# The last expert of each mixture layer is weighted in one operation and scattered by itself

## The chip, the cores and the metric

The kernel runs on one core of a Trainium2 chip. A core has a matrix engine (PE; its weight loads are listed apart as PEld), a vector engine (DVE), a scalar engine (ACT), a general engine (POOL), a queue engine (SP) and 16 DMA engines. Each engine works through its own list of instructions in order. The metric is the time of one execution on the device, in microseconds (us); the median of several executions counts.

## The reference, cut to what matters

Two transformer blocks are computed in float32 on 256 tokens of width 1024 (and 256 context tokens). The second block has two layers, l = 0 and l = 1, and each ends in a mixture of 16 experts. Every expert takes its 32 best tokens, runs them through its own three matrices, and adds the gated result back to those tokens:

```python
gate, idx = lax.top_k(jnp.swapaxes(aff, 1, 2), cap)      # cap = 32 of 256 tokens
xe = h[bidx, idx]
hid = jax.nn.silu(xe @ w1) * (xe @ w3)                    # per expert
ye = (hid @ w2) * gate[..., None]
return jnp.zeros_like(h).at[bidx, idx].add(ye)            # and x = x + g2 * this
...
x = x + g2 * expert_choice_ffn(h2, ...)
if need_ctx: xc = xc + g2c * expert_choice_ffn(hc2, ...)  # layer 0 only
return rms_norm(x, final_norm)
```

In layer 0 the experts run for two streams, x and the context xc (`ns == 2`). In layer 1 they run for x alone (`ns == 1`), and the block ends with the norm.

## The kernel before

The function `moe` builds a mixture layer and `run` executes it. A loop runs over the 16 experts. Each needs 12 MB of weights (w1, w3, w2, four transfers of 1 MB each, tile `wm`), loaded through a ring of buffers by SP. The products with them (`ps_a<-wm,xe`, `ps_a<-wm,xf`, `ps_a<-wm,hidT`) use groups of the array's columns: 64 columns per stream pair in layer 0 (two products side by side), 32 in layer 1 (four side by side). `hid` (L1325) is the gated hidden state, made when w1 and w3 of an expert are done; its transpose `hidT` feeds w2; the result of w2 stands in `py`, with 32 rows for each part of the width and each stream.

L1344 multiplies `py` by the layer's gate vector G2 into the tile `ye`, in four operations of 32 rows, because each expert has its own 32 rows of `ye` (four experts fill 128 rows). After every fourth expert `gates(qt)` builds the four experts' scatter matrix: a comparison on DVE (L1228, tile `Pg`), a product on POOL (L1230), transposes on PE, and a copy to `PgT`. The scatter then multiplies `PgT` and `ye` over all 128 rows, 512 columns at a time (`ps_b<-ye,PgT`): eight products in layer 0 and four in layer 1. L1360 adds them to the streams on DVE. In layer 0 each group of four is added to x and xc at once; in layer 1 the four groups gather in four banks `acc`, and the add comes behind the last group, at e == 15.

Behind layer 0 comes the odd layer's input: `normed` squares xc and x on ACT (L447), makes `rs` on POOL (L439) and `xn` on ACT and DVE (L170, L172); `mod_T` transposes `xn` on PE and splits the result into `oT` on ACT, DVE and POOL (L472 to L477). The first weights of that layer (`w<-in_odd_w_in`) are split on ACT and DVE or POOL (`wh`, L203, L205). Behind layer 1 comes the final norm (L1833 to L1840): squares on ACT, products with the norm's weights on POOL (first half of the tokens) and DVE (second half), `rs` on POOL, a scaling (L170, L172), and the stores.

The order of the instructions on each engine is set by a scheduler which simulates the program when it is built, not by the order of the code alone. Two helpers, `evac` and `scaled`, take ACT and DVE in turn, so one more call changes the engine of every later one.

Of the kernel before, what the change touches and what calls it, by code (L numbers as in the profile page):

```python
# [27 lines left out]
OP = mybir.AluOpType  # L28
# [85 lines left out]
def kernel(ctx, tc, A, out, dbg=None):  # L114
    nc = tc.nc
    dbg = dbg or {}
    V, S, G, PE = nc.vector, nc.scalar, nc.gpsimd, nc.tensor
# [19 lines left out]
    def ps_(tag):  # L137
        return PS["pool"].tile([128, 512], F32, name="ps_" + tag, tag=tag, bufs=PS["n"][tag])

    def psa():  # L140
        return ps_("a")

    def psb():
        return ps_("b")
# [3 lines left out]
    def mm(o, l, r, start=True, stop=True, **kw):  # L148
        PE.matmul(o, l, r, start=start, stop=stop, **kw)  # L149
# [3 lines left out]
    def evac(o, i):  # L153
        flip_eng[0] ^= 1
        if flip_eng[0]:
            S.activation(o, i, AF.Copy)
        else:
            V.tensor_copy(o, i)
# [19 lines left out]
    def bcast(ap, shape):  # L178
        return ap.to_broadcast(shape)
# [73 lines left out]
    def tr(o, i):  # L253
        n = i.shape[0]
        PE.transpose(o, i, ident[:n, :n])  # L255
# [120 lines left out]
    def in_pairs(j, n=128):  # L376

        c = 256 * (j // 2) + j % 2
        return slice(c, c + 2 * n - 1, 2)
# [790 lines left out]
    def moe(l, streams, stk):  # L1170

        ns = len(streams)
        nj = 4 // ns
        W = 32 * ns
        N = 1024 // nj
# [19 lines left out]
        G2 = SC.rearrange("p a b c -> p (a b c)")[:, 0:N]  # L1195
# [3 lines left out]
        def chosen(part, of=tuple(reversed(range(ns)))):  # L1199

            if part not in xe:
                inputs(part)
                P = mp.tile([128, ns, 2, 4, 32], F32, name="P", tag="P")
                for s in range(ns):
                    Ps[s, part] = P[:, s]
            for s in of:
                P = Ps[s, part]
                for t in range(2):
                    V.tensor_tensor(P[:, t], bcast(iota1[:, None, :], [128, 4, 32]),
                                    bcast(POS[s][:, t, 4 * part:4 * part + 4, None], [128, 4, 32]), op=OP.is_equal)  # L1210
                    V.tensor_scalar(P[:, t], P[:, t], QS[s][:, t:t + 1], None, op0=OP.mult)

        def gather(s, part, k, ps=None):

            ps = (ps_("g" if ns == 2 else "a")[:, 0:128] if ps is None else ps).rearrange("p (e w) -> p e w", w=32)
            for t in range(2):
                mm(ps, streams[s][:, t, in_pairs(k)], Ps[s, part][:, t], start=t == 0, stop=t == 1)
            affine(xe[part][:, k, :, 32 * s:32 * s + 32], ps, MS[:, i_sc, k, s:s + 1], shift[:, k, s:s + 1])

        def gates(qt):  # L1220

            p = psa() if ns == 1 else psb()
            for s in range(ns):
                Pg = rowp.tile([128, 512], F32, name="Pg", tag="r")
                for t in range(2):
                    g_ = Pg[:, 128 * t:128 * t + 128].rearrange("p (e w) -> p e w", w=32)
                    e4 = slice(4 * qt, 4 * qt + 4)
                    V.tensor_tensor(g_, bcast(iota1[:, None, :], [128, 4, 32]),  # L1228
                                    bcast(POS[s][:, t, e4, None], [128, 4, 32]), op=OP.is_equal)
                    G.tensor_tensor(g_, g_, bcast(AFF[s][:, t, e4, None], [128, 4, 32]), op=OP.mult)  # L1230
                    tr(p[:, 256 * s + 128 * t:256 * s + 128 * t + 128], Pg[:, 128 * t:128 * t + 128])
            PgT = rowp.tile([128, 512], F32, name="PgT", tag="r")
            evac(PgT[:, 0:256 * ns], p[:, 0:256 * ns])
            return PgT
# [29 lines left out]
        def ffn(lhs, src, before=None, last=False):  # L1264
            ps = psa()
            for kk in range(4):
                w = load_m(src, 2 * kk, last and kk == 3)
                for k in range(2):
                    if before and 2 * kk + k + 1 < 8:
                        before(2 * kk + k + 1)  # L1270
                    for j in range(nj):
                        mm(ps[W * j:W * j + W, :N], lhs(2 * kk + k), w[:, k, N * j:N * j + N],
                           start=kk == 0 and k == 0, stop=kk == 3 and k == 1)
            return ps
# [11 lines left out]
        def run():  # L1286
            yes = {}
            if ns == 1:
                acc = [psb() for j in range(4)]

            def work(name, n):
                return rowp.tile([128, 512], F32, name=name, tag="r")[:, :n]

            chosen(0, (0,))


            late = [(s, part, k) for part in ((1, 3, 2) if ns == 2 else (1, 2, 3)) for k in range(8) for s in range(ns)]
            turn = [0.0]

            def first(k):  # L1300
                if k < 7:
                    gather(0, 0, k + 1)

            def more(_):
                if late and e >= ((0, 1, 4, 3) if ns == 2 else (0, 1, 1, 1))[late[0][1]]:
                    turn[0] += 0.8
                    if turn[0] >= 1.0:
                        turn[0] -= 1.0
                        s, part, k = late.pop(0)
                        if part not in xe:  # L1310
                            chosen(part)
                        gather(s, part, k)

            gather(0, 0, 0)
            first(0)
            for e in range(16):
                def xk(k):
                    return xe[e // 4][:, k, e % 4]

                hook = more if e else first  # L1320
                p1 = ffn(xk, A["moe_w1_2"][l, e], hook)
                hid = work("hid", N)
                S.activation(hid, p1[:, :N], AF.Silu)  # L1323
                p3 = ffn(xk, A["moe_w3_2"][l, e])
                V.tensor_tensor(hid, hid, p3[:, :N], op=OP.mult)  # L1325
                nblk = N // 128
                pt = psa() if ns == 1 else ps_("t")
                for c in range(nblk):
                    tr(pt[:, 128 * c:128 * c + 128], hid[:, in_pairs(c)])
                hidT = work("hidT", N).rearrange("p (c w) -> p c w", c=nblk)  # L1330
                evac(hidT, pt[:, :N].rearrange("p (c w) -> p c w", c=nblk))

                py = ffn(lambda K: hidT[:, K % nblk, W * (K // nblk):W * (K // nblk) + W], A["moe_w2_2"][l, e],
                         more, last=e == 15)
                if e == 0:
                    gate2()
                if e == 0 or ns == 2 and e % 4 == 0:
                    xe["y"] = mp.tile([128, 2048], F32, name="ye", tag=("ye", "xf2")[e // 4 % 2])
                    ye = yes[e // 4] = xe["y"].rearrange("p (s n) -> p s n", s=2)
                o = 32 * (e % 4)  # L1340
                for j in range(nj):
                    for s in range(ns):
                        i = 32 * (ns * j + s)
                        V.tensor_tensor(ye[o:o + 32, s, N * j:N * j + N], py[i:i + 32, :N], G2[i:i + 32, :], op=OP.mult)  # L1344

                qt = (e + 1) // 4 - 1 if ns == 1 or e > 5 else 0
                if e % 4 < 3 and (ns == 1 or e != 5) or ns == 2 and e == 3:
                    continue
                assert ns == 1 or not late
                PgT = gates(qt)  # L1350
                for s in reversed(range(ns)):
                    for t in range(2):
                        for h in range(2):
                            ps = acc[2 * t + h] if ns == 1 else psb()
                            mm(ps, PgT[:, 256 * s + 128 * t:256 * s + 128 * t + 128],
                               yes[qt if ns == 2 else 0][:, s, 512 * h:512 * h + 512],
                               start=ns > 1 or e == 3, stop=ns > 1 or e == 15, skip_group_check=ns == 1)
                            if ns > 1 or e == 15:
                                d = streams[s][:, t, 512 * h:512 * h + 512]
                                V.tensor_tensor(d, d, ps, op=OP.add)  # L1360
            stk.close()

        return run, gts, apart_, slots, ahead


# [500 lines left out]
```

## Time and profile before

| what | us |
|---|---|
| median of 3 runs | 1858.48 (1857.36 to 1864.18) |
| profiled execution, its own time | 1863.53 |
| its span, first to last instruction | 1861.5 |
| layer 0's experts, last `ye` starts at | 1213.47 |
| layer 1's experts, last `ye` starts at | 1847.13 |

A row of the time line gives the start, the time it took, the engine, the line of the code, the operation, the tiles (result first, operands behind the arrow), the shape and the number of instructions merged; in brackets stands the idle time of the engine before it and what ended it. A float32 product is recorded as two matmul instructions. The profile's page shows PE busy for 88% of the span, DVE for 40%, ACT for 26% and POOL for 18%; the DMA engines move about 420 GB/s through both layers' experts.

### The profile page before, as it was taken

To read this page: it belongs to the slowest core of one execution; us is meant where nothing else is said; L and a number is where in the kernel's file an instruction comes from. 1 tells how busy PE (TensorE), PEld (TensorE's weight loads), DVE (VectorE), ACT (ScalarE), POOL (GpSimd) and SP (SyncE) were. 2 spreads that over 40 slices of the span, in tenths; PEclk is the share of its full clock that TensorE was granted. 3 is DMA by queue.
4 is the path that set the end of the run, shared out by engine and by line. 5 is a ranking of instruction groups with operands and counts; after the bars stand their busy time and mean duration, and the time that the engine had idled before them with its cause. 6 is when DMAs were issued, how large, how long until landed. Compare 5 with 4: busy or idle time off the path is not lost.

```text
span 1861.5 us, 29005 instructions
## 1 busy us (share of the span) xinstructions
PE 1632.1 (88%) x12102; PEld 1040.2 (56%) x12102; DVE 753.7 (40%) x1490; ACT 480.9 (26%) x938; POOL 336.0 (18%) x291
## 2 busy tenths in 40 slices
PE   5999999999999999999999999889997976666665
PEld 4787877889888778533433333368775522222221
DVE  3538888857644574321222121164653200000002
ACT  4335545635534343100100000062441100000001
POOL 4105534742422521000000000031310000000001
PEclk8999999989999999999999999999998977776777
DMA  9566544546566737899999999962187999999996
GB/s 351 183 222 231 179 135 143 201 147 205 168 227 200 229 138 280 339 385 410 421 412 420 420 420 420 419 197 74 69 358 298 423 424 426 425 425 425 425 424 274
DMA packets 173191, 557.12 MB, mean 299 GB/s; under 512 B 22579, under 2 KB 79271, under 8 KB 124164
## 3 DMA queue, kind: packets, MB, share of 16 engines
q1 hardware_dynamic: 166688, 547.92, 75.9%
q10 hardware_dynamic: 5732, 6.33, 1.0%
q8 instruction: 95, 1.56, 0.3%
q0 software_dynamic: 640, 1.02, 0.1%
q14 instruction: 36, 0.29, 0.0%
HBM read 554.18 MB, written 1.05 MB: 298 GB/s over the span
## 4 chain that ended last, share of the span: by engine, by line
PE 53%; DMA 34%; DVE 7%; ACT 3%; issue 2%; POOL 1%; SPq 0%; POOLq 0%; DVEq 0%; ACTq 0%
PE ps_a L149 42%; DMA wm<-in_moe_w_dram 27%; PE ps_b L149 6%; PE ps_b L255 3%; DMA w<-in_even_w_in_dram 2%; DMA w<-in_w_in_dram 2%; PE ps_g L149 2%; DVE w L827 1%; DMA w<-in_even_w_out_dram 1%; DVE wh L205 1%; ACT wh L203 1%; DMA w<-in_w_ada_dram 1%; DMA w<-in_odd_w_in_dram 1%; DVE acc L641 0%; DVE wh L786 0%
## 5 line engine op out<-in xcount | busy, mean ns | idle before, releaser
L149 PE MATMUL ps_a<-wm,xe 128*64 128x512 f32 (+1 forms) x1536 | 268.0, 528 | 1.6 <-DMA wm<-in_moe_w_dram 1.6
L149 PE MATMUL ps_a<-wm,hidT 128*32 128x256 f32 (+1 forms) x1536 | 205.3, 509 | 43.3 <-DMA wm<-in_moe_w_dram 26.0
L203 ACT ACTIVATE wh<-w 128x1024 fp32r<-128x1024 f32 (+3 forms) x152 | 151.5, 1007 | 178.7 <-PE ps_a L149 95.8
L149 PEld LDWEIGHTS ps_a<-wm,xe 128*64 128x64 f32 (+1 forms) x1536 | 90.2, 128 | 151.8 <-issue 130.6
L205 DVE TENSOR_TENSOR wh<-w,wh 128x1024 fp32r<-128x1024 f32 (+3 forms) x102 | 135.7, 1334 | 92.4 <-ACT wh L203 92.1
L205 POOL TENSOR_TENSOR wh<-w,wh 128x1024 fp32r<-128x1024 f32 (+3 forms) x50 | 115.3, 2307 | 317.0 <-ACT wh L203 292.4
L1325 DVE TENSOR_TENSOR hid<-hid,ps_a 128x512 f32<-128x512 f32 (+1 forms) x32 | 17.8, 555 | 366.1 <-PE ps_a L149 366.1
L149 PEld LDWEIGHTS ps_a<-wm,hidT 128*32 128x32 f32 (+1 forms) x1536 | 69.3, 130 | 151.9 <-issue 78.1
L1344 DVE TENSOR_TENSOR ye<-ps_a,SC 32x512 f32<-32x512 f32 (+1 forms) x128 | 70.8, 553 | 196.0 <-PE ps_a L149 194.5
L149 PE MATMUL ps_a<-wm,xf 128*32 128x256 f32 x1024 | 98.5, 522 | 55.7 <-DMA wm<-in_moe_w_dram 55.7
L149 PE MATMUL ps_a<-hT,wh 128*128 128x512 f32 (+1 forms) x672 | 138.4, 362 | 5.8 <-ACT hT L522 4.3
L1230 POOL TENSOR_TENSOR Pg<-Pg,BC 128x128 f32<-128x128 f32 x24 | 9.4, 415 | 727.8 <-DVE Pg L1228 727.8
L1323 ACT ACTIVATE hid<-ps_a 128x512 f32<-128x512 f32 (+1 forms) x32 | 15.7, 491 | 456.3 <-PE ps_a L149 456.3
L149 PEld LDWEIGHTS ps_a<-hT,wh 128*128 128x128 f32 x672 | 112.2, 199 | 26.1 <-ACT hT L522 4.7
L149 PE MATMUL ps_a<-E,wh 128*128 128x256 f32 x768 | 104.7, 292 | 6.9 <-DVE wh L205 2.3
L149 PE MATMUL ps_a<-wh,E 128*128 128x256 f32 (+1 forms) x576 | 102.1, 327 | 5.0 <-ACT wh L203 2.8
L149 PEld LDWEIGHTS ps_a<-E,wh 128*128 128x128 f32 x768 | 97.6, 195 | 13.2 <-ACT E L476 2.6
L149 PEld LDWEIGHTS ps_a<-wm,xf 128*32 128x32 f32 x1024 | 35.0, 137 | 118.1 <-DMA wm<-in_moe_w_dram 67.2
L149 PEld LDWEIGHTS ps_a<-wh,E 128*128 128x128 f32 x576 | 82.1, 189 | 18.9 <-issue 4.8
L149 PE MATMUL ps_a<-wm,ye 128*32 128x256 f32 x512 | 49.7, 530 | 24.2 <-DMA wm<-in_moe_w_dram 24.2
L641 DVE SCALAR_TENSOR_TENSOR acc<-ps_a,CV,acc 128x189 f32<-128x189 f32 (+2 forms) x160 | 66.8, 428 | 8.4 <-ACT acc L630 5.9
L149 PE MATMUL ps_a<-w,SC 128*32 128x128 f32 x1728 | 66.1, 286 | 3.5 <-DMA w<-in_w_ada_dram 2.1
(527 smaller groups left out, 2362.8 us busy)
## 6 DMA issues: line engine op xcount, KB each, us to landing
wm<-in_moe_w_dram SPq DMA_DIRECT2D x382, 1024.0 KB, 19.5
w<-in_ada_w_dram SPq DMA_DIRECT2D x46, 1024.0 KB, 6.7
w<-in_even_w_in_dram SPq DMA_DIRECT2D x24, 1024.0 KB, 7.3
w<-in_w_ada_dram SPq DMA_DIRECT2D x12, 1024.0 KB, 8.2
w<-in_w_in_dram SPq DMA_DIRECT2D x8, 1024.0 KB, 8.5
w<-in_even_w_out_dram SPq DMA_DIRECT2D x8, 1024.0 KB, 8.5
w<-in_w_in_dram SPq DMA_DIRECT2D x12, 512.0 KB, 6.4
w<-in_w_in_dram SPq DMA_DIRECT2D x8, 768.0 KB, 4.4
```

What stands on the lines that cost most here:

```text
L149: PE.matmul(o, l, r, start=start, stop=stop, **kw)
L203: S.activation(hv, wv, AF.Copy)
L205: (G if flip_lo[0] == 0 else V).tensor_tensor(lo, wv, hv, op=OP.subtract)
L255: PE.transpose(o, i, ident[:n, :n])
L641: V.scalar_tensor_tensor(o, xi[:, r0 + dr:r1 + dr, c0 + dc:c1 + dc], tap(i, j), o, op0=OP.mult, op1=OP.add)
L827: V.scalar_tensor_tensor(w[:, r], cb[:, c, 1], dt[:, c, 24 + h:25 + h], w[:, r], op0=OP.mult, op1=OP.add)
L1230: G.tensor_tensor(g_, g_, bcast(AFF[s][:, t, e4, None], [128, 4, 32]), op=OP.mult)
L1323: S.activation(hid, p1[:, :N], AF.Silu)
L1325: V.tensor_tensor(hid, hid, p3[:, :N], op=OP.mult)
L1344: V.tensor_tensor(ye[o:o + 32, s, N * j:N * j + N], py[i:i + 32, :N], G2[i:i + 32, :], op=OP.mult)
```

## The change

In `run`, expert 15 leaves its group. The last group holds experts 12 to 14, and its scatter (96 rows) moves from behind expert 15 to behind expert 14; in layer 1 the four banks `acc` are added to x there. A second call, `gates(None, 15)`, builds the scatter matrix of expert 15 four times over, once for each quarter of the array's rows. At the end one operation weights all 128 rows of `py` (`y15`), and products on 32 rows each, at four positions of the array's rows, scatter it; for each of the two token tiles there are four products, with 512 columns in layer 0 and 256 in layer 1, followed by an add each.

```diff
-        def gates(qt):
+        def gates(qt, e=None):
...
-                    e4 = slice(4 * qt, 4 * qt + 4)
+                    e4 = slice(4 * qt, 4 * qt + 4) if e is None else slice(e, e + 1)
...
+                if e == 15:
+                    break
...
-                qt = (e + 1) // 4 - 1 if ns == 1 or e > 5 else 0
-                if e % 4 < 3 and (ns == 1 or e != 5) or ns == 2 and e == 3:
+                qt = {3: 0, 7: 1, 11: 2, 14: 3}.get(e) if ns == 1 else {5: 0, 7: 1, 11: 2, 14: 3}.get(e)
+                if qt is None:
                     continue
+                K = 96 if qt == 3 else 128
                 PgT = gates(qt)
+                if e == 14:
+                    PgE = gates(None, 15)
...
-                               start=ns > 1 or e == 3, stop=ns > 1 or e == 15, skip_group_check=ns == 1)
-                            if ns > 1 or e == 15:
+                               start=ns > 1 or e == 3, stop=ns > 1 or e == 14, skip_group_check=ns == 1)
+                            if ns > 1 or e == 14:
                                 d = streams[s][:, t, 512 * h:512 * h + 512]
                                 V.tensor_tensor(d, d, ps, op=OP.add)
+            y15 = work("y15", N)
+            V.tensor_tensor(y15, py[:, :N], G2, op=OP.mult)
+            for t in range(2):
+                if ns == 1:
+                    pss = [psa() for j in range(4)] if t else acc
+                else:
+                    pss = [ps_("bbgg"[i]) for i in range(4)]
+                parts = [(s, j) for s in reversed(range(ns)) for j in range(nj)]
+                for s, j in parts:
+                    i = 32 * (ns * j + s)
+                    mm(pss[nj * s + j][:, :N], PgE[i:i + 32, 256 * s + 128 * t:256 * s + 128 * t + 128], y15[i:i + 32],
+                       tile_position=(i, 0))
+                for s, j in parts:
+                    d = streams[s][:, t, N * j:N * j + N]
+                    V.tensor_tensor(d, d, pss[nj * s + j][:, :N], op=OP.add)
```

The new code moves instructions at three places. First, PE at the end of layer 0, from expert 14's w2 on. Before:

```order
L149 MATMUL ps_a<-wm,hidT 64x512 x16
L149 MATMUL ps_a<-wm,xe 64x512 x32
L255 MATMUL ps_t<-kb,hid 128x128 x4
L149 MATMUL ps_a<-wm,hidT 64x512 x4
L255 MATMUL ps_b<-kb,Pg 128x128 x3
L149 MATMUL ps_a<-wm,hidT 64x512 x4
L255 MATMUL ps_b<-kb,Pg 128x128
L149 MATMUL ps_a<-wm,hidT 64x512 x8
L149 MATMUL ps_b<-ye,PgT 128x512 x8
```

And now, from the last quarter of expert 14's w2 on (eight transposes `ps_b<-kb,Pg` stand in the three quarters before):

```order
L149 MATMUL ps_a<-wm,hidT 64x512 x4
L149 MATMUL ps_a<-wm,xe 64x512 x4
L149 MATMUL ps_b<-ye,PgT 128x512 x3
L149 MATMUL ps_a<-wm,xe 64x512 x4
L149 MATMUL ps_b<-ye,PgT 128x512 x3
...
L149 MATMUL ps_a<-wm,xe 64x512 x16
L255 MATMUL ps_t<-kb,hid 128x128 x4
L149 MATMUL ps_a<-wm,hidT 64x512 x16
L149 MATMUL ps_g<-y_9605,PgT 128x512 x2
L149 MATMUL ps_b<-y_9605,PgT 128x512 x3
L149 MATMUL ps_g<-y_9605,PgT 128x512 x2
L149 MATMUL ps_b<-y_9605,PgT 128x512
```

The eight scatter products stand now among expert 15's w1 products, and behind its w2 stand the eight products on quarters of the rows (`y_9605` is `y15`). Second, ACT at the same place, between expert 15's `hid` and the first `mod_T`. Before:

```order
L1560 DMA ko<-in_k_odd_dram 128x552
L203 ACTIVATE wh<-w 128x832 x4
L447 ACTIVATE xn_9604,ss_9605<-xc 128x1024 x2
L447 ACTIVATE xn_9669,ss_9670<-x 128x1024
L170 ACTIVATE xn_9604<-xc,rs 128x1024
```

And now:

```order
L1582 DMA ko<-in_k_odd_dram 128x552
L1587 DMA wu<-in_mla_w_uq_dram 128x2x768
L1591 DMA wu<-in_mla_w_ukv_dram 128x8x64 x2
L203 ACTIVATE wh<-w 128x832 x2
L447 ACTIVATE xn_9643,ss_9644<-xc 128x1024
L203 ACTIVATE wh<-w 128x832 x2
L447 ACTIVATE xn_9708,ss_9709<-x 128x1024
L447 ACTIVATE xn_9643,ss_9644<-xc 128x1024
L447 ACTIVATE xn_9708,ss_9709<-x 128x1024
L170 ACTIVATE xn_9643<-xc,rs 128x1024
L170 ACTIVATE xn_9708<-x,rs 128x1024
```

Two of the four splits of the odd layer's first weights stand now behind a square of xc, and both streams' squares stand ahead of both scalings. Third, ACT at the program's end. Before:

```order
L1833 ACTIVATE o,ss<-x 128x512 x4
L170 ACTIVATE o<-o,rs 128x512
L1840 DMA out_dram<-o 128x512
L170 ACTIVATE o<-o,rs 128x512
L1840 DMA out_dram<-o 128x512
```

And now:

```order
L1855 ACTIVATE o,ss<-x 128x512 x3
L170 ACTIVATE o<-o,rs 128x512
L1855 ACTIVATE o,ss<-x 128x512
L1862 DMA out_dram<-o 128x512
L170 ACTIVATE o<-o,rs 128x512
L1862 DMA out_dram<-o 128x512
```

The scaling of the first token tile stands now ahead of the last square of the second.

## Rows read from the trace of the kernel before

**Rows 1.** The page, chain of work that ended last: shares by engine.

```profile
PE 53%; DMA 34%; DVE 7%; ACT 3%; issue 2%; POOL 1%; SPq 0%; POOLq 0%; DVEq 0%; ACTq 0%
```

**Rows 2.** Stretches: length, busy time of five engines, granted PE clock, DMA share, GB/s.

```profile
1106.49:1129.07 22.58, 22.43 (x82) 6.72 (x78) 8.26 (x12) 0.60 (x1) 0.00 (x0) 1.00 1.01 421
...
1244.60:1248.30 3.70, 0.00 (x0) 0.00 (x0) 2.58 (x7) 2.64 (x13) 3.59 (x3) 1.00 0.87 253
1248.40:1251.80 3.40, 3.40 (x16) 3.12 (x17) 2.69 (x9) 0.40 (x2) 1.06 (x3) 0.50 0.19 36
1404.00:1418.00 14.00, 5.68 (x30) 4.70 (x28) 7.88 (x29) 0.88 (x3) 2.78 (x3) 0.55 0.54 225
1700.00:1800.00 100.00, 66.34 (x663) 24.07 (x656) 7.55 (x19) 2.31 (x6) 0.76 (x2) 0.74 1.01 425
```

**Rows 3.** Time line of DVE, layer 0: experts 11, 12, 14 and 15.

```profile
1096.60 0.69 DVE L1325 TENSOR_TENSOR hid<-hid,ps_a 128x512 f32<-128x512 f32 x1 [11.01 <-PE ps_a L149]
...
1106.71 2.81 DVE L1344 TENSOR_TENSOR ye<-ps_a,SC 32x512 f32<-32x512 f32 x4 [4.62 <-PE ps_a L149]
...
1129.18 0.69 DVE L1325 TENSOR_TENSOR hid<-hid,ps_a 128x512 f32<-128x512 f32 x1 [6.41 <-PE ps_a L149]
...
1177.30 0.69 DVE L1325 TENSOR_TENSOR hid<-hid,ps_a 128x512 f32<-128x512 f32 x1 [11.02 <-PE ps_a L149]
1186.66 2.79 DVE L1344 TENSOR_TENSOR ye<-ps_a,SC 32x512 f32<-32x512 f32 x4 [8.68 <-PE ps_a L149]
1202.97 0.69 DVE L1325 TENSOR_TENSOR hid<-hid,ps_a 128x512 f32<-128x512 f32 x1 [13.52 <-PE ps_a L149]
...
1213.47 2.81 DVE L1344 TENSOR_TENSOR ye<-ps_a,SC 32x512 f32<-32x512 f32 x4 [7.27 <-PE ps_a L149]
```

**Rows 4.** Time line of PE, layer 0: scatter behind expert 11, and expert 15's w3.

```profile
1108.31 3.25 PE L149 MATMUL ps_b<-ye,PgT 128*128 128x512 f32 x6
...
1195.94 1.94 PE L149 MATMUL ps_a<-wm,xe 128*64 128x512 f32 x8 [0.47 <-DMA wm<-in_moe_w_dram]
```

**Rows 5.** Time lines of ACT and DVE behind layer 0's experts.

```profile
1213.13 1.68 ACT L203 ACTIVATE wh<-w 128x832 fp32r<-128x832 f32 x2 [2.66 <-DMA w<-in_odd_w_in_dram]
...
1216.31 0.69 DVE L1360 TENSOR_TENSOR xc<-xc,ps_b 128x512 f32<-128x512 f32 x1
1216.91 1.02 DVE L205 TENSOR_TENSOR wh<-w,wh 128x832 fp32r<-128x832 f32 x1
...
1218.57 1.06 ACT L447 ACTIVATE xn<-xc 128x1024 f32<-128x1024 f32 x1 [0.86 <-DVE xc L1360]
...
1226.31 1.02 ACT L472 ACTIVATE r<-ps_b,M,MS 128x256 f32<-128x256 f32 x2 [0.62 <-DVE r L474]
...
1228.72 1.15 ACT L170 ACTIVATE xn<-x,rs 128x1024 f32<-128x1024 f32 x1
...
1235.87 0.63 ACT L476 ACTIVATE oT<-r 128x512 fp32r<-128x512 f32 x1
```

**Rows 6.** Time line of PE, odd layer: products on two halves of the array's rows.

```profile
1326.09 1.14 PE L149 MATMUL ps_a<-rqT,rkT 64*128 64x256 f32 x8
```

**Rows 7.** Time lines of all engines at the program's end.

```profile
1847.13 1.75 DVE L1344 TENSOR_TENSOR ye<-ps_a,SC 32x256 f32<-32x256 f32 x4 [8.03 <-PE ps_a L149]
...
1848.13 3.67 PE L149 MATMUL ps_b<-ye,PgT 128*128 128x512 f32 x8 [1.06 <-DVE ye L1344]
...
1849.26 0.69 DVE L1360 TENSOR_TENSOR x<-x,ps_b 128x512 f32<-128x512 f32 x1 [0.38 <-PE ps_b L149]
...
1849.98 0.63 ACT L1833 ACTIVATE o<-x 128x512 f32<-128x512 f32 x1 [8.28 <-DVE x L1360]
...
1850.78 1.27 POOL L1834 TENSOR_TENSOR o<-x,fw 128x512 f32<-128x512 f32 x1 [10.97 <-ACT o L1833]
...
1855.78 0.56 POOL L439 TENSOR_TENSOR rs<-ms,misc 128x1 f32<-128x1 f32 x1 [0.66 <-DVE ms L436]
...
1856.37 0.72 ACT L170 ACTIVATE o<-o,rs 128x512 f32<-128x512 f32 x1 [0.50 <-POOL rs L439]
```

More of the change, by code (lines that the diff above doesn't have):

```diff
@@ L1354, in run @@
                             ps = acc[2 * t + h] if ns == 1 else psb()
-                            mm(ps, PgT[:, 256 * s + 128 * t:256 * s + 128 * t + 128],
-                               yes[qt if ns == 2 else 0][:, s, 512 * h:512 * h + 512],
-                               start=ns > 1 or e == 3, stop=ns > 1 or e == 15, skip_group_check=ns == 1)
-                            if ns > 1 or e == 15:
+                            mm(ps, PgT[0:K, 256 * s + 128 * t:256 * s + 128 * t + 128],
+                               yes[qt if ns == 2 else 0][0:K, s, 512 * h:512 * h + 512],
+                               start=ns > 1 or e == 3, stop=ns > 1 or e == 14, skip_group_check=ns == 1)
+                            if ns > 1 or e == 14:
                                 d = streams[s][:, t, 512 * h:512 * h + 512]
                                 V.tensor_tensor(d, d, ps, op=OP.add)
+            y15 = work("y15", N)
[13 more added lines that the diff above has]
+                    V.tensor_tensor(d, d, pss[nj * s + j][:, :N], op=OP.add)
             stk.close()
```

## The prediction

> **What bounds the kernel now.** I read the chain that ended last first: PE holds 53% of the span and the DMA engines 34%, all others little [rows 1]. So a piece on DVE, ACT or POOL counts only where neither covers it. Then I read the stretches. In layer 1's experts the DMA engines are busy without a break (share 1.01) and PE only for 66 of 100 us [rows 2]: PE work that is moved there between the weights is hidden, and what counts is the tail behind the last weights. Layer 0 looks alike on the page, but isn't. While expert 12's w1 and w3 run, PE is busy for 22.43 of 22.58 us, with the DMA share at 1.01 too [rows 2]: the weights were fetched far ahead, and PE works off what has piled up. Only in expert 15's w3 has PE caught up; it waits about 0.5 us for each of the last three transfers (one of three rows: 0.47) [rows 4]. So PE work put ahead of that point is hidden only as far as these waits, and all of it that is not delays the end of layer 0. From there the delay travels on: between the two layers' experts, at 1404 to 1418 us, the DMA share is down to 0.54 [rows 2], because the buffers are full and wait for layer 1's first products. A later layer 0 means a later start of the last DMA-bound stretch, and a later end, one for one.
>
> **The change part by part.**
>
> *Scatter of experts 12 to 14 moved ahead, layer 0.* The trace holds this very pattern one group earlier: behind expert 11 come four transposes, and eight scatter products stand among expert 12's w1. From `hid` to `hid`, expert 12 takes 1129.18 - 1096.60 = 32.58 us [rows 3]. Expert 15, which has none of this before it, takes 1202.97 - 1177.30 = 25.67 [rows 3]. With the new order, expert 15 gets expert 12's interval. The products themselves are dearer than they look: six records, three products, stand for 3.25 us [rows 4].
>
> *Four more transposes for the second scatter matrix.* From `hid` to `ye` expert 11, with four transposes inside w2, takes 1106.71 - 1096.60 = 10.11 us, and expert 14, without, 1186.66 - 1177.30 = 9.36 [rows 3]: 0.75 us for four. Eight stand now in expert 14's w2, four of them contained in the 32.58. So `hid` of expert 15 falls at 1177.30 + 32.58 + 0.75 = 1210.63, which is 7.66 later. Its w2 is free of transposes now and takes 9.36 instead of 10.50 (1213.47 - 1202.97 [rows 3]). The last expert's result is weighted from 1219.99 instead of 1213.47: **6.5 us later**. Weights don't hold it up, the last of them come in before 1213.13, when the odd layer's, queued behind them, are there [rows 5].
>
> *Behind layer 0: one weighting, products on quarters, adds.* Before, from 1213.47 the order is four weightings (2.81), the scatter, eight adds, and the odd layer's input; ACT's last `oT` ends at 1235.87 + 0.63 = 1236.50 [rows 3, 5], 23.0 us later. Now one weighting of 0.69 (as an add of that size) ends at 1220.7. The first add before came 1.13 after its product's start, and 0.14 is lost in the handing over (1849.26 - 1848.13 in the last layer, where the second quarter of the weighting had ended at 1847.99 by the steps of 0.43 to 0.44 in 1.75) [rows 7]. So the first add starts at 1222.0. Two adds at 0.64 a piece, the step of queued ones (estimate from 0.69 with some overlap), end at 1223.3. Then ACT squares xc (1.06 and the reading of the sum, together about 1.25) until 1224.6, and only behind that splits the third piece of the weights (0.84, half of 1.68) until 1225.4 [rows 5]. DVE needs that piece for its second split (1.02) [rows 5], which ends at 1226.4; five adds of 0.64 follow, to 1229.6. ACT squares the halves as they come, to 1231.5, scales `xn` twice (1.15 each) to 1233.8, and has eight `r` (0.51 each) and eight `oT` (0.63 each) left, 9.1 us [rows 5]: 1242.9, **6.4 us later** than before. What the shorter weighting gains, 2.1 us, is spent by the split and the second square that now stand ahead of the input's scaling. I carry 6.5. Bounds: the row before has 16.4 us from 1213.47 to the end of the scaling of x (1228.72 + 1.15 [rows 5]) and the new order 13.8; if ACT didn't set the end, 2.6 would come back. If xc's way alone set it, some 1.4 more would be lost.
>
> *Products on quarters.* No product on 32 rows stands in the trace; the nearest are on 64 rows at two positions, eight records or four products of 256 columns in 1.14 us [rows 6]. A full product of 512 columns is about 0.92 with its tail (3.67 for four [rows 7]), so four of 256 one after another would take about 1.75. They run side by side, and I take the same for four quarters: 0.86 for 512 columns, 0.43 for 256. The Trainium skill (TensorE: Matmul & The Clock Gate, "Measured speedup vs the span model") gives four row tiles 3.07 times the speed, not four; by it each group in layer 0 would be dearer by an estimated 0.3 us, and the sum by at most 0.6.
>
> *Layer 1: scatter moved ahead.* Two gate builds, four products and four adds stand now between expert 14 and 15, where PE has about 34 us of slack in 100 [rows 2]: nothing, unless that cover is gone, and then some 4 us.
>
> *The tail.* Before, the first add starts at 1849.26 [rows 7]. Now one weighting of 0.42 from 1847.13, 0.14 for handing over, and a product of half the columns with its way to DVE, about 0.70, make 1848.4: 0.9 earlier. Four adds of about 0.44 finish the first tile at 1850.1. ACT's first square (0.63 and the reading) lets POOL begin at 1850.1 instead of 1850.78; two products of 1.27 end at 1852.6, and `rs` (0.56) at 1853.2 [rows 7]. But on ACT the first tile's scaling (0.72) stands now ahead of the last square. That square ends with its reading at 1854.8, DVE multiplies (about 0.7), sum and scale take 0.3, `rs` 0.56: the last scaling starts at 1856.4, and before it started at 1856.37 [rows 7]. So the tail's gain is eaten by the order, **0.0**; bounds -0.9, all of the earliness kept, and +0.5, a step of waiting more.
>
> *Turns of ACT and DVE.* One more `evac` in each layer changes the engine of all copies in the odd layer. Copies differ by about 0.1 us between the engines; with some twenty on the path I allow 2 us either way, and take nothing.
>
> **Sum.** 6.5 + 0.0 = +6.5 us. Made against the profiled execution, 1863.53 + 6.5 = 1870.0; that execution lies 5.05 above the median of the runs shown, so the median to expect is 1858.48 + 6.5 = **1865.0 us**, 0.35% above. Half a per cent, 9.3 us, is about what a measurement of this kernel can tell from no change.
>
> **The rivals.**
>
> *A, the moved scatter is hidden.* If the waits for weights in expert 15's w3 were only the visible part of PE's slack, the products would cost nothing and the earlier weighting would pay: 2.1 less behind layer 0 and up to 0.9 less in the tail, 1858.48 - 3.0 = 1855.5. For it speaks the DMA share of 1.01 all through layer 0, against it that PE is busy for 22.43 of 22.58 us there [rows 2] and that its waits come to some 1.6 us, three times the row's 0.47 to 0.56.
>
> *B, slower: PE's clock falls behind layer 0.* PE would stand idle from about 1226, after the last product on quarters, to 1232.6, when `xn` of xc is there. The trace has an idle PE from 1244.6 to 1248.3, and right behind it a granted clock of 0.50, that is 1.2 GHz, for 3.4 us of full work; around 1404 to 1418 it stands at 0.55 [rows 2]. Before the change no gap so long lies behind layer 0. [...] Its price is 1.7 us for one such stretch of dense work, and up to 4 where the transposes that feed ACT run slowly too; with 3.5 the sum is +10.0, 1868.5 us, slower by 0.54%.
>
> *C, the quarters don't run side by side.* Eight products of 0.86 in a row would feed eight adds of 0.64 in layer 0, but two splits stand between the adds, so 1 to 2 us appear; in the tail four of 0.43 match the adds' pace. About 1866.5 us. The pair rows speak against it [rows 6].
>
> **How the numbers follow.** Forecast 0.62, A 0.12, B 0.18, C 0.08. The low end takes from the forecast the 2.6 behind layer 0, the 0.9 of the tail and the 2 of the turns, -5.5, and with the chance of A cut by half it lies at 1858.5. The high end takes 6.5 + 1.4 + 0.5 and 2 of the turns, 10.4, and holds B's likely part: 1870.5. More than half a per cent slower (above 1867.8) are most of B and the forecast's upper margin: 0.21. Faster by as much (under 1849.2) would need the moved work hidden and the odd layer shorter: 0.02. The rest, 0.77, is within.
>
> **What would show it.** In the profile of the changed kernel: `hid` of expert 15 in layer 0 comes 33 us behind that of expert 14, not 26; PE has no wait for weights in its w3. The row of the weighting (one operation, 128 rows) starts near 1220, and ACT's last `oT` ends near 1243. At the end, four 32-row products start within some ns of each other and eight adds of about 0.44 follow, while ACT's last square waits for a scaling. The prediction is wrong if expert 15's interval stays at 26 us, if the DMA share between the layers shows that the delay was taken up before layer 1's weights, or if the odd layer itself is longer or shorter by more than 2 us.

## The result

| kernel | median, us | runs |
|---|---|---|
| before | 1859.69 | 6 (1856.55 to 1864.18) |
| after | 1871.8 | 6 (1867.4 to 1875.91) |

The change made the kernel slower: the ratio is 1.0069, with a 95% interval of 1.0047 to 1.0092, some 12 us. The forecast was 1865.0 us, in a range that ended at 1870.5. The direction was right, the size was half of what came, and the time lies 1.3 us outside the range.

Whole times of one program differ by up to 16 us between executions (before, over all the comparisons here: 1850.7 to 1866.9), so the comparison goes by rows: by stretches between the same instructions of both traces. Each landmark is the start of one instruction: `hid` of layer 0's expert 0 (e0) and 15 (e15), the weighting of expert 15, the first transposes of the odd layer's latents, its first score product (`ps_a<-kT,qT`), the first transposes of its result (`kb,Yo`), the first `hid` of layer 1, the weighting of layer 1's expert 15, and the end of the last scaling (behind it come only the stores). All numbers are us from one profiled execution of each kernel. The kernels from the third row on are the experiments below.

| kernel | e0 to e15 | to weighting | to latents | to scores | to Yo | to layer 1 | to its last weighting | to the end | sum |
|---|---|---|---|---|---|---|---|---|---|
| before | 412.47 | 10.50 | 34.86 | 74.91 | 48.99 | 60.56 | 414.34 | 9.96 | 1066.6 |
| after | 420.84 | 11.14 | 34.22 | 73.43 | 57.21 | 59.29 | 414.25 | 10.02 | 1080.4 |
| turn_back | 420.86 | 9.36 | 34.29 | 73.57 | 49.00 | 60.57 | 414.47 | 10.02 | 1072.1 |
| before_flip | 413.28 | 12.07 | 33.69 | 74.88 | 57.39 | 60.58 | 414.61 | 9.90 | 1076.4 |
| fill_gap | 417.46 | 9.44 | 34.24 | 73.43 | 50.11 | 59.58 | 414.32 | 10.12 | 1068.7 |
| layer1_only | 412.49 | 10.48 | 34.86 | 74.83 | 48.98 | 60.58 | 414.52 | 9.29 | 1066.0 |
| no_scatter | 412.67 | 9.71 | 36.51 | 73.54 | 48.98 | 60.57 | 414.38 | 10.02 | 1066.4 |
| fill_l0 | 419.17 | 9.37 | 33.83 | 75.83 | 47.46 | 60.63 | 414.24 | 10.02 | 1070.6 |
| l1_fill | 412.51 | 10.49 | 34.87 | 74.80 | 49.03 | 60.56 | 414.28 | 9.31 | 1065.9 |
| sst_act | 420.86 | 11.14 | 34.25 | 73.43 | 58.78 | 60.56 | 414.05 | 10.03 | 1083.1 |
| tail_turn | 420.85 | 9.38 | 34.27 | 73.53 | 49.04 | 60.58 | 414.20 | 10.02 | 1071.9 |

After against before: +8.4 up to `hid` of expert 15, which was forecast (7.7), +8.2 in the odd layer between the first score product and `Yo`, which was not, and -1.5 and -1.3 in the two stretches around the latter.

### The profile page after: what moved, and what is told of

It is laid out like the page before. It is cut to its first block, busy times and chain, and to the rows that moved or that the text cites. A ratio compares the mean times of both kernels' runs of the same rounds, so it can differ in the third digit from the quotient of the medians.

```text
span 1865.6 us, 29103 instructions
## 1 busy us (share of the span) xinstructions
PE 1642.2 (88%) x12140; PEld 1045.6 (56%) x12140; DVE 765.6 (41%) x1507; ACT 481.4 (26%) x939; POOL 338.5 (18%) x297
## 4 chain that ended last, share of the span: by engine, by line
PE 64%; DMA 24%; DVE 7%; ACT 2%; issue 2%; POOL 1%; SPq 0%; DVEq 0%; POOLq 0%; ACTq 0%
PE ps_a L149 50%; DMA wm<-in_moe_w_dram 19%; PE ps_b L149 7%; PE ps_b L255 3%; DMA w<-in_w_in_dram 2%; PE ps_g L149 2%; DVE w L827 1%; DMA w<-in_even_w_in_dram 1%; DMA w<-in_w_ada_dram 1%; ACT wh L203 1%; DVE wh L205 1%; DMA w<-in_even_w_out_dram 1%; PE ps_t L255 1%; DVE hid L1326 1%; DVE acc L641 0%
## 5 line engine op out<-in xcount | busy, mean ns | idle before, releaser
L149 PE MATMUL ps_a<-wm,hidT 128*32 128x256 f32 (+1 forms) x1536 | 210.7, 524 | 37.1 <-DMA wm<-in_moe_w_dram 19.9
L149 PE MATMUL ps_a<-wm,xf 128*32 128x256 f32 x1024 | 93.1, 500 | 53.5 <-DMA wm<-in_moe_w_dram 53.5
L1347 DVE TENSOR_TENSOR ye<-ps_a,SC 32x512 f32<-32x512 f32 (+1 forms) x120 | 66.4, 553 | 179.5 <-PE ps_a L149 173.5
```

## The profile after

The end of layer 0 came as predicted. These are rows of DVE's time line in the changed kernel, `hid` of expert 14, `hid` of expert 15 and the one weighting (the rows of before are in [rows 3]):

```profile
1167.41 0.69 DVE L1326 TENSOR_TENSOR hid<-hid,ps_a 128x512 f32<-128x512 f32 x1 [11.02 <-PE ps_a L149]
...
1201.48 0.69 DVE L1326 TENSOR_TENSOR hid<-hid,ps_a 128x512 f32<-128x512 f32 x1 [6.41 <-PE ps_a L149]
...
1212.62 0.69 DVE L1369 TENSOR_TENSOR y<-ps_a,SC 128x512 f32<-128x512 f32 x1 [8.92 <-PE ps_a L149]
```

From `hid` to `hid` it takes 34.07 us instead of 25.67. PE's time line at the same place shows why, and what stands behind:

```profile
1185.65 2.84 PE L149 MATMUL ps_b<-ye,PgT 96*128 96x512 f32 x6
...
1203.79 8.78 PE L149 MATMUL ps_a<-wm,hidT 128*64 128x512 f32 x32 [0.83 <-issue]
1213.36 0.70 PE L149 MATMUL ps_g<-y,PgT 32*128 32x512 f32 x2 [0.79 <-DVE y L1369]
1213.38 0.70 PE L149 MATMUL ps_b<-y,PgT 32*128 32x512 f32 x2
1213.90 0.59 PE L149 MATMUL ps_g<-y,PgT 32*128 32x512 f32 x2
1213.91 1.45 PE L149 MATMUL ps_b<-y,PgT 32*128 32x512 f32 x4
...
1224.62 1.75 PE L255 MATMUL ps_b<-kb,xn 128*128 128x128 f32 x7 [5.78 <-ACT xn L170]
```

The scatter of experts 12 to 14 stands among expert 15's w1; no wait for weights is left there. The products on quarters start within 0.02 us of each other, in groups of four. Then PE stands idle for 5.78 us. ACT's last `oT` ends at 1234.92, 22.30 behind the weighting (23.0 before):

```profile
1234.29 0.63 ACT L476 ACTIVATE oT<-r 128x512 fp32r<-128x512 f32 x1
```

The surprise is in the odd layer. PE's rows around the first transposes of a softmax row, after the change:

```profile
1323.12 1.13 PE L149 MATMUL ps_a<-rqT,rkT 64*128 64x256 f32 x8
1327.71 1.11 PE L255 MATMUL ps_b<-kb,pr 128*128 128x128 f32 x4 [3.45 <-ACT pr L1050]
1328.62 1.92 PE L149 MATMUL ps_a<-kT,qT 96*128 96x512 f32 x2
```

and the same place before:

```profile
1326.09 1.14 PE L149 MATMUL ps_a<-rqT,rkT 64*128 64x256 f32 x8
1327.77 1.13 PE L149 MATMUL ps_a<-kT,qT 96*128 96x512 f32 x2 [0.55 <-ACT sst L156]
1330.01 0.86 PE L255 MATMUL ps_b<-kb,pr 128*128 128x128 f32 x4 [1.11 <-ACT pr L1050]
```

Before, a score product (`ps_a<-kT,qT`) stood in the time in which ACT and DVE make the softmax row `pr`. After, the transposes of `pr` stand ahead of that product, and PE waits 3.45 us in one piece. What follows is seen in the stretches (PE's busy time comes first, the granted clock stands ahead of the DMA share), after:

```profile
1310.00:1327.29 17.29, 14.26 (x114) 11.44 (x112) 12.56 (x14) 9.58 (x14) 9.46 (x7) 1.00 0.22 87
1327.29:1344.36 17.07, 16.65 (x52) 11.02 (x53) 6.84 (x14) 4.19 (x11) 3.87 (x7) 0.50 0.16 62
```

and before:

```profile
1313.00:1330.31 17.31, 15.66 (x117) 11.81 (x116) 13.02 (x15) 11.40 (x18) 8.96 (x6) 1.00 0.30 99
1330.31:1333.72 3.41, 3.41 (x13) 1.87 (x12) 2.39 (x7) 1.46 (x4) 2.93 (x6) 0.50 0.67 276
```

Before, the clock stood at 0.50 (1.2 GHz) for 3.4 us. After, it stood there for 17.1 us, of which PE was busy for 16.65. Half of 17.1 less half of 3.4 is 6.8 us of lost work, and 8.2 were lost in the stretch.

In the tail, PE and ACT after the change (the rows of before are in [rows 7]):

```profile
1851.50 0.71 PE L149 MATMUL ps_b<-y,PgT 32*128 32x256 f32 x8 [0.55 <-DVE y L1369]
1852.04 0.61 PE L149 MATMUL ps_a<-y,PgT 32*128 32x256 f32 x8
```

```profile
1857.33 0.72 ACT L170 ACTIVATE o<-o,rs 128x512 f32<-128x512 f32 x1 [2.27 <-POOL rs L439]
1857.96 0.61 ACT L1855 ACTIVATE o<-x 128x512 f32<-128x512 f32 x1
```

Two groups of four products follow each other by 0.54 us, and on ACT the last square (L1855) stands behind the first tile's scaling (L170), as the prediction had it.

## The experiments

A turn is one call of a helper that takes ACT and DVE by turns (`evac`, `scaled`, and a third, `affine`); the bit `flip_eng` holds whose turn it is. The first theory after the comparison: one more `evac` in each layer swaps ACT and DVE for the copies of the odd layer, the scheduler then orders PE's work differently, PE gets a gap, and the gap brings the long half clock. The main rival: the idle PE behind layer 0 brings it, whoever makes the copies.

**turn_back.** The changed kernel with the turn restored.

```diff
                 if e == 14:
                     PgE = gates(None, 15)
+                    flip_eng[0] ^= 1
```

> The changed kernel, with the turn of ACT and DVE set back by one behind the extra scatter matrix, so that every copy of the odd layer falls to the engine that had it before. Theory (the turns): in the changed kernel the copy of sst falls to DVE, the scheduler puts the transposes of the first softmax row ahead of the next score product, PE idles 3.45 us, and its granted clock then stands at 0.50 for 17 us; with the turn set back the score product stands ahead again, the gap is at most 1.2 us, no long stretch at 0.50 follows, and from the first latents to the first hid of layer 1 the time is that of before, 184.5 us (changed kernel: 189.9). The whole is 6.5 to 8.5 us slower than before (ratio 1.0035 to 1.0045), not 12. Rival (what layer 0's end does to the clock): the long stretch at half clock comes from the idle PE behind layer 0, whoever makes the copies; then it stays, the odd layer still takes about 190 us, and the whole stays at 12 (1.0065).

Measured: ratio to before 1.0026 (1.0011 to 1.0040), +4.8 us; from the first score product to `Yo` 49.00 us, as before. PE's rows and the stretch behind them:

```profile
1320.52 1.13 PE L149 MATMUL ps_a<-kT,qT 96*128 96x512 f32 x2 [0.55 <-ACT sst L156]
1322.76 0.85 PE L255 MATMUL ps_b<-kb,pr 128*128 128x128 f32 x4 [1.11 <-ACT pr L1050]
```

```profile
1323.10:1326.50 3.40, 3.40 (x12) 1.82 (x11) 2.41 (x6) 1.42 (x4) 2.90 (x6) 0.50 0.69 289
```

The score product is back at its place, and the half clock lasts 3.4 us. The gap behind layer 0 is still there, so the rival falls. The median is a little below the range expected, its interval reaches into it; by the rows the kernel is 5.5 us longer than before.

**before_flip.** The kernel before, with the turn alone.

```diff
+            flip_eng[0] ^= 1
             stk.close()
 
         return run, gts, apart_, slots, ahead
```

> The kernel before, with nothing but the turn of ACT and DVE moved on by one behind each layer's experts. Layer 0 and its scatter are as before. Theory (the turns): the gap of some 3.4 us in front of the first softmax transposes and the long stretch at 0.50 behind it appear here too, from the first latents to the first hid of layer 1 it takes about 190 us, and the whole is 5.5 us slower than before (ratio 1.0030, between 1.002 and 1.004). Rival (layer 0's end): no such stretch, 184.5 us, ratio 1.0000 within 0.001.

Measured: ratio 1.0026 (1.0008 to 1.0044), +4.8 us, without any of the new code. The gap and the long half clock are there:

```profile
1327.36 0.66 PE L255 MATMUL ps_b<-kb,pr 128*128 128x128 f32 x4 [3.45 <-ACT pr L1050]
```

```profile
1328.70:1345.80 17.10, 17.10 (x62) 12.79 (x62) 5.21 (x10) 3.06 (x8) 2.29 (x6) 0.50 0.11 46
```

From scores to `Yo` it takes 57.39 us. A side finding: up to expert 15's weighting this kernel has before's instructions, and yet w2 of expert 15 took 1.6 us longer (12.07 against 10.50), with the clock at 0.50 from 1202.4 for 3.4 us. Such a short fall comes and goes between executions.

**fill_gap.** The changed kernel with its swapped turns; three idle products are put into the gap.

```diff
+        if fill is not None:
+            for i in range(3):
+                mm(fill[0:1, :], mx, rv[:, 0, 0:512])
         pr = wp.tile([128, 512], F32, name=name, tag="pr", bufs=npr)
...
-                pr, su = softmax_p(op_, ps, 512, scale, "pr", 2)
+                pr, su = softmax_p(op_, ps, 512, scale, "pr", 2, po if t == 0 and h == 0 else None)
```

> The changed kernel, with three idle products (1 x 512, results overwritten) that wait for the first softmax row's maximum and stand in the gap of 3.45 us in the odd layer; turns and the other copies stay as changed. Theory (the gap makes the half clock, the half clock makes the time): the longest PE gap there falls to about 1 us, the granted clock stays at 1.00 or has one short fall behind it, and from the first latents to the first hid of layer 1 it takes 182 to 186 us instead of 190; the whole is 5 to 9 us slower than before. Rival (the new order itself is longer, the clock only goes along): 189 to 191 us, and the whole stays at 12.

Measured: ratio 1.0024 (1.0010 to 1.0038), +4.5 us, a little under the 5 to 9 expected; 50.11 us from scores to `Yo`. PE, and the stretch behind:

```profile
1320.19 2.74 PE L149 MATMUL ps_b<-rv,mx 128*1 128x512 f32 x6 [0.77 <-DVE mx L1045]
1322.86 0.70 PE L149 MATMUL ps_a<-rqT,rkT 64*128 64x256 f32 x2
1323.49 0.66 PE L255 MATMUL ps_b<-kb,pr 128*128 128x128 f32 x4
```

```profile
1322.00:1339.00 17.00, 17.00 (x113) 12.20 (x111) 9.32 (x20) 7.11 (x21) 5.55 (x10) 1.00 0.18 64
```

More work for PE, and the stretch is 7.1 us shorter: the clock stays at 1.00. So most of the price of the swapped order, 7.1 of the 8.2 us, is the half clock, and the half clock comes with the gap. (With the old order and no half clock in this stretch, in fill_l0 below, it takes 47.46 us; the 2.65 more here are about what the fillers take, 2.74.) The fillers also shifted some products behind them, so this is not the gap alone; but the transposes of `pr` still stand ahead of the next score product, as in the changed kernel. (The sum in the table is smaller than the ratio says, because this execution was 3.4 us shorter in layer 0's experts, which is told at the end.)

**sst_act.** In the first wording the copy of `sst`, which had fallen to DVE, was the cause. Here this copy alone goes back to ACT.

```diff
-        evac(sst, ps.rearrange("p (d a v) -> p d a v", d=2, a=2))
+        flip_eng[0] ^= 1
+        S.activation(sst, ps.rearrange("p (d a v) -> p d a v", d=2, a=2), AF.Copy)
```

> The changed kernel, with the copy of sst alone given back to ACT; all other turns stay as changed, and PE's instructions stand in the changed kernel's order. Theory now (PE's order makes the gap, not the engine of this one copy): PE still waits 3.45 us for the first softmax row, the long stretch at 0.50 follows, and from the first score product to the transposes of Y it takes 56 to 58 us (57.2 as changed, 49.0 before). Rival (my first wording: the copy of sst on DVE is what matters): the gap is under 3 us, no long stretch, 50 us or less.

Measured, in one execution: 58.78 us from scores to `Yo`, with the gap, and half clock for even longer.

```profile
1337.13 1.12 PE L255 MATMUL ps_b<-kb,pr 128*128 128x128 f32 x4 [3.45 <-ACT pr L1050]
```

```profile
1336.50:1357.00 20.50, 19.87 (x68) 14.24 (x68) 6.45 (x13) 5.52 (x13) 4.27 (x8) 0.50 0.14 51
```

The gap goes with PE's order, which the swapped turns as a whole bring about. Which of the copies turns it stays open; this one alone doesn't.

**layer1_only.** The change in layer 1 alone.

```diff
-                if e == 15:
+                if e == 15 and ns == 1:
                     break
...
-                qt = {3: 0, 7: 1, 11: 2, 14: 3}.get(e) if ns == 1 else {5: 0, 7: 1, 11: 2, 14: 3}.get(e)
+                qt = {3: 0, 7: 1, 11: 2, 14: 3}.get(e) if ns == 1 else {5: 0, 7: 1, 11: 2, 15: 3}.get(e)
...
+            if ns == 2:
+                stk.close()
+                return
             y15 = work("y15", N)
```

> The change in layer 1 alone; layer 0 and the odd layer keep their instructions. Theory: the moved scatter and the second matrix are hidden behind layer 1's weights, and the tail gives back what the earlier add gains because the first tile's scaling stands ahead of the last square: 0.0 us from the last weighting to the last scaling (9.2 us before), and a ratio of 1.0000 within 0.0007. Rival: the moved products hold up the weights' buffers in layer 1, up to 4 us, ratio 1.002.

Measured: ratio 0.9993 (0.9979 to 1.0007), no difference. The stretch of layer 1's experts is 414.52 us (414.34 before): the moved scatter is hidden. But the tail is 0.67 us shorter, not equal. ACT's rows:

```profile
1844.72 0.63 ACT L1858 ACTIVATE o<-x 128x512 f32<-128x512 f32 x1 [2.16 <-DVE x L1385]
...
1845.35 0.71 ACT L170 ACTIVATE o<-o,rs 128x512 f32<-128x512 f32 x1
```

Here the last square stands ahead of the first tile's scaling, and what the quarters gain in the tail arrives at the end.

**tail_turn.** I took the turns for the cause of that, since layer1_only has one extra turn when the final norm comes. So turn_back got one more turn there.

```diff
     fn = enter(name="fin", bufs=1, side="right", reuse_waits="tile")
+    flip_eng[0] ^= 1
```

> The changed kernel with the turn set back behind the extra matrices, and moved on by one ahead of the final norm, so that the first tile's first scaling falls to DVE and the last square on ACT need not wait for it. Theory (the tail's gain is eaten by that scaling ahead of the last square): from the last weighting to the end 9.3 us, as with the change in layer 1 alone, instead of 10.0. Rival (the 9.3 there came from something else): 9.9 to 10.1.

Measured, in one execution: 10.02 us, the rival. The turn gives ACT the other half of the tile, but the last square still stands behind it:

```profile
1852.87 0.72 ACT L170 ACTIVATE o<-o,rs 128x512 f32<-128x512 f32 x1 [2.26 <-POOL rs L439]
...
1853.50 0.61 ACT L1857 ACTIVATE o<-x 128x512 f32<-128x512 f32 x1
```

Of the nine kernels here with quarters in layer 1, the two that leave layer 0 alone (layer1_only, l1_fill) have the square ahead and end 9.3 us behind the weighting; the seven others have it behind and take 10.0 to 10.1. Why the scheduler chose so isn't settled; the turn alone isn't it.

**no_scatter.** What the moved scatter costs in layer 0, by leaving it out.

```diff
                 if e == 14:
                     PgE = gates(None, 15)
+                    flip_eng[0] ^= 1
+                if ns == 2 and e == 14:
+                    continue
```

> The changed kernel with the turn set back, and without the scatter of experts 12 to 14 in layer 0: its eight products and eight adds are left out, so these three experts' results are missing from both streams. Theory (the moved products delay expert 15 one for one): from hid of expert 14 to hid of expert 15 it takes 26 to 27 us instead of 34.06 (25.68 before, and four more transposes than there), and from hid of expert 14 to the end 7 to 8 us less than with the turn set back (685.4). Rival (the interval is set by weights that come later, or by the adds' buffers): 30 us or more, and less than 4 us at the end.

Measured, in one execution: `hid` to `hid` 25.87 us, so the eight products cost 8.2 us there. The sum is only 5.7 less than with turn_back, where 7 to 8 were expected, since 2.2 are lost again behind the weighting (36.51 against 34.29 us to the latents). A row of ACT names the new bound:

```profile
1211.14 1.68 ACT L203 ACTIVATE wh<-w 128x832 fp32r<-128x832 f32 x2 [10.64 <-DMA w<-in_odd_w_in_dram]
```

The odd layer's weights come last now. Of the 8 us that the scatter takes, about 2 would have been waited for anyway.

**fill_l0.** My rival B was a fall of the clock behind layer 0. The clock did fall there: in the changed kernel it stood at 0.50 from 1218.06 on, for 10.24 us:

```profile
1218.06:1228.30 10.24, 4.46 (x19) 3.68 (x18) 7.38 (x14) 8.00 (x13) 3.40 (x3) 0.50 0.66 203
```

To price it, idle products fill PE behind the quarters of turn_back.

```diff
                     V.tensor_tensor(d, d, pss[nj * s + j][:, :N], op=OP.add)
+                if ns == 2:
+                    spare = spare if t else ps_("t")
+                    for i in range(3):
+                        mm(spare, streams[1][:, t, 0:128], y15)
```

> The changed kernel with the turn set back, and six idle products behind layer 0 (128 x 512, result not used; three wait for the first adds to xc, three for the third) that fill the gap before the first transposes. Theory (the gap lowers the clock there, but ACT and DVE set the pace, so it costs next to nothing): the stretch at 0.50 of 10 us is gone or cut to one of 3.4, and from the last weighting to the first latents it still takes 33.8 to 34.6 us (34.3). Rival (the fall costs what my forecast's rival B gave it): 1.5 to 3.5 us less, 31 to 32.8.

Measured: the clock stays up, and PE's wait for `xn` is cut:

```profile
1213.00:1219.00 6.00, 5.54 (x22) 2.04 (x22) 4.31 (x7) 2.73 (x4) 0.25 (x1) 1.00 0.94 246
1219.00:1225.00 6.00, 3.80 (x15) 1.72 (x13) 3.93 (x8) 4.46 (x7) 3.01 (x3) 1.00 0.99 311
```

From weighting to latents it takes 33.83 us, 0.46 less. But the half clock came later instead, at the latents:

```profile
1245.60:1252.40 6.80, 5.85 (x26) 5.21 (x27) 3.25 (x10) 0.55 (x3) 2.80 (x4) 0.50 0.74 229
```

From there to the scores it takes 75.83 us, 2.3 more than in turn_back, and from the scores to `Yo`, with no half clock, 1.5 less; from the weighting to `Yo` it is 157.1 us in fill_l0 and 156.9 in turn_back. So the fall behind layer 0 is real, and taking it away there gained nothing on the way to `Yo`: PE was busy for only 4.46 of its 10.24 us. Over the whole (ratio 1.0014, 1.0001 to 1.0027) it can't be told from turn_back.

**l1_fill.** Since a gap is dear in the odd layer, the two gaps at layer 1's start [rows 2] were filled on top of layer1_only.

```diff
+        if l == 1:
+            for i in range(2):
+                mm(lt[0:16, :], RWS[s][:, 0], src[:, 0, 0:512])
...
+        if l == 1:
+            for i in range(4):
+                mm(lt[0:16, :], aff[:, 0], src[:, 0, 0:512])
```

> The change in layer 1 alone, and six idle products (16 x 512, results not used) in the two gaps of PE while layer 1's tokens are chosen. Theory (a half clock behind a gap costs time wherever PE is the bound, the start of layer 1's experts too): the granted clock is back at 1.00 before the first gather, the first hid of layer 1 follows the router's sum by 22 to 23.5 us instead of 24.8, and the end comes 1.5 to 3 us earlier than with the change in layer 1 alone (ratio to before 0.998). Rival (the choice of the tokens or the weights set the pace there): 24.5 to 25 us, no gain.

Measured: ratio 0.9987 (0.9971 to 1.0002), which can't be told from layer1_only; from the router's sum to the first `hid` 24.96 us, no gain. The condition failed: the clock had fallen at 1397.4, ahead of the fillers, and it fell again at 1411.1, at the first gathers. The fillers themselves ran slowly, two products in 3.60 us:

```profile
1400.06 3.60 PE L149 MATMUL ps_a<-x,kb 128*16 128x512 f32 x4 [0.38 <-DVE BC L1137]
```

They also stood in the way: the choice of the tokens begins 4.51 us behind the router's sum instead of 3.39 in layer1_only. So this run doesn't tell whether a full clock would help there.

## Why the prediction was wrong, point by point

- **The moved scatter, layer 0: right, for an execution like that of the trace.** The forecast was 33.33 us from `hid` to `hid` of expert 15, and 34.07 came (34.07 in turn_back too). The place, the cause and the missing waits for weights were as told; no_scatter gives the 8.2 back. But the price depends on how far PE is behind the weights. Before, after and turn_back were traced with three short falls of the clock between e0 and expert 14's `hid` (last section). before_flip, whose layer 0 is that of before, had one, and its PE came 3.4 us earlier to that point (383.41 us from e0 instead of 386.80). It then waited for all eight transfers of expert 15's w1 and w3, not for three; the first and the last:

```profile
1179.88 1.94 PE L149 MATMUL ps_a<-wm,xe 128*64 128x512 f32 x8 [0.64 <-DMA wm<-in_moe_w_dram]
...
1197.22 1.94 PE L149 MATMUL ps_a<-wm,xe 128*64 128x512 f32 x8 [0.56 <-DMA wm<-in_moe_w_dram]
```

So `hid` of expert 15 came no earlier (413.28 us after e0, before 412.47): in the five traces without the moved scatter this stretch takes 412.5 to 413.3. With it, each fall less shows: 420.84 us with three, 419.17 with two (fill_l0), 417.46 with one (fill_gap). With one fall on both sides the scatter costs 4.2 us (fill_gap against before_flip), not 8.4.

- **Expert 15's w2: right, but for chance.** The forecast was 9.36 us; turn_back has 9.36. The profiled execution of the changed kernel has 11.14, with a short fall of the clock in it (at 1204.41, for 3.4 us); fill_gap, with the same code up to there, has 9.44, and before_flip shows such a fall without the change.
- **Behind layer 0: right.** The forecast was 22.9 us from the weighting to ACT's last `oT`, 22.3 came. Of the Trainium skill's figure for four row tiles (TensorE: Matmul & The Clock Gate, "Measured speedup vs the span model") the tail can say something. One group of four products of 256 columns follows the other by 0.54 us, where four in a row would take 4 x 0.43: 3.2 times. But that step begins with a start after a wait. The second group's eight records last 0.61 us together and 0.374 each, so its second record of each product starts about 0.22 us behind the first: with two records to a product, four products in full stride take some 0.43 us, as long as one. That is four times, as I took it, and not the page's 3.07. It changed nothing, for DVE's adds are slower.
- **One gain was left out.** In the new order PE idles 2.43 us in front of the latents (2.54 in turn_back), not 3.74, and the short half clock of before at 1248.40 [rows 2] is gone: from latents to scores turn_back takes 1.3 us less.
- **Layer 1's scatter and the tail: right.** 414.25 us instead of 414.34, and 10.02 instead of 9.96, with the last square behind the scaling. layer1_only shows that the bound of -0.9 was a real one: with the square ahead, 0.67 are gained.
- **Rival B: the sign was right, its place and its price wrong.** I had the fall behind layer 0, with 1.7 to 4 us. It came there, and without it the latents came 0.5 us earlier (fill_l0). I looked for it behind the longest gap, but the gap that cost most had 3.45 us; and 1.7 us was the price of the shortest stretch only, though [rows 2] had 14 us at 0.55 too.
- **"Turns of ACT and DVE": this step failed.** I reckoned the swap as some twenty copies of about 0.1 us, allowed 2 us, and took nothing. It isn't the copies' own length. (PE's order in the odd layer moves too; it is missing among the three places named with the change.) The scheduler lays out PE's work by simulated times, and with the turns swapped it puts the transposes of the first `pr` ahead of a score product; PE idles 3.45 us there instead of 0.55 and 1.11; and its clock stands at half for 17.1 us of nearly full work. before_flip prices this at +4.8 us by medians (+1.5 to +8.2) and +8.4 by the stretch, where I had allowed 2; turn_back, which is the change as my sum described it, at +4.8 (+2.0 to +7.4), +5.5 by the rows, where my sum said +6.5. The two together give 9.6 by medians, within the interval of the whole (+8.7 to +17.1), and 13.9 by rows, where after less before is 13.8.

The sum by rows is above that by medians. Part of this can come from layer 0: the traces of before, after and turn_back have three short falls there, and in an execution with fewer the moved scatter costs less. That alone doesn't explain before_flip, with 8.4 by the stretch against 4.8 by medians; each kernel has one trace, so this stays open.

No version here beats the kernel before by what can be measured. layer1_only is 0.6 us shorter by rows, with a ratio of 0.9993.

## What to carry to other kernels

Where a build-time scheduler and alternating helpers set the order, one more call early in the program is a change to all that follows: compare the order of the bound engine in every later stage, not only where the code was edited, and look for work that no longer fills a wait. Price a new gap on a matrix engine not by its length but by what stands behind it: dense work at half clock for as long as the trace shows such a stretch to last. And move work ahead only up to the point where the engine already runs without waiting for data; here it was hidden in layer 1, where PE waits for weights, and cost 8.4 us in layer 0, where PE waited for 1.6 us in all, and 4.2 where the clock had left it more to wait for. One trace shows only one such case.

## What was not expected of the hardware

The half clock can last far longer than the gap that preceded it, while PE is busy all the time: 17.1 us with PE busy for 16.65 (after), 17.10 of 17.10 (before_flip), 20.5 with 19.87 (sst_act), each behind a gap of 3.45 us. Products on 64 and 96 rows and transposes are among the work in these stretches. Filled to 0.77 us, the gap left the clock at 1.00 for the same work (fill_gap). What lets the clock rise again in these stretches wasn't tested.

In layer 0's experts the clock falls to 0.50 for 3.4 us at a few places (in the trace of before at 1026.5, 1074.3 and 1132.3), with PE busy all through:

```profile
1132.30:1135.70 3.40, 3.40 (x10) 0.95 (x8) 0.00 (x0) 0.00 (x0) 0.00 (x0) 0.51 1.01 422
```

Between executions with the same instructions there, their number changes: three in before, one in before_flip, and e0 to expert 14's `hid` takes 386.80 and 383.41 us (385.08 with two falls, in l1_fill). So each is worth some 1.7 us up to there. Without the moved scatter that is lost again to the wait for weights; with it, it reaches the end of layer 0. Most of what tells whole times apart lies elsewhere: e0 itself comes at 777.91 us (turn_back) to 790.50 (before) from the start of the span, though no edit touches what stands ahead of layer 0's experts. What makes that difference stays open.
